# A first quarter in three pieces, and dummy products among the token transposes

## The chip, the core and the metric

The kernel runs on one core of a Trainium2 chip. The core has a matrix engine (PE, with its own loader of stationary operands, PEld), a vector engine (DVE), an activation engine (ACT), a general engine (POOL) and a queue engine (SP); SP, ACT and POOL can issue DMAs, which sixteen DMA engines carry out. The metric is the time of one execution in microseconds (us). Three executions of the kernel before took 2226.09, 2226.78 and 2231.04 us; the median is 2226.78 us.

## What is computed

One step of a two-layer trunk for 128 prompt tokens and 512 sample tokens with 2048 features. In each layer every token is normalised, scaled and shifted by a modulation that depends on its group's conditioning vector, sent through one wide input projection, a mixer, and an output projection:

```python
def modulation(cond, w, b):
    m = jax.nn.silu(cond) @ w + b
    ...
    return jnp.split(m, 3, axis=-1)
...
    for layer in range(DEPTH):
        sh_p, sc_p, gt_p = modulation(c_ctx, ada_w[layer], ada_b[layer])
        sh_s, sc_s, gt_s = modulation(c, ada_w[layer], ada_b[layer])
        hp = rms_norm(xp, norm_g[layer]) * (1.0 + sc_p) + sh_p
        hs = rms_norm(xs, norm_g[layer]) * (1.0 + sc_s) + sh_s
        ...
            out_p, (kc, vc) = even_mixer(hp, *w)
            out_s, _ = even_mixer(hs, *w, ctx=(cache_a_k[:, i], cache_a_v[:, i]), rope=rope)
```

`ada_w` has 2048 x 6144 numbers a layer: columns 0 to 2047 give the shift, the next 2048 the scale, the last 2048 the gate. So the first product of the input projection cannot start before the tokens are transposed, their norms are known, and at least some columns of `ada_w[0]` have been read and multiplied with the two conditioning vectors.

## The kernel before

**Layout.** Tokens stand along the free dimension (640 columns: 512 sample and 128 prompt tokens), features along the 128 partitions; the 2048 features are 16 feature tiles, four of which are a quarter (`qd`). A wide product of the projection takes three passes (weights high by tokens high, high by low, low by high; lines 364 to 366), each over 320 tokens, so a feature tile costs one output tile six matmuls.

**The start.** `x_load` fetches the tokens in five blocks of two halves (line 120), on ACT's queue and SP's. `x_block` (line 1072) sends each block through PE: four transposes fill one PSUM bank `T` (line 1078; two such banks in turn), DVE or, for the last of the four groups of every other block, ACT copies it to `xT` (line 1079), and ACT squares and sums the block's halves for the norms (line 1083). POOL raises the sums to the power -1/2, and `x_rows` spreads them (lines 1093 and 1094).

**Conditioning.** `ada_on_pe(l, cb, j0, n)` makes `n` feature tiles of column block `cb` of the modulation: 16 weight tiles with 32 x (n*128) products (line 195) into a bank `T`, a copy by ACT to `ada_sb` (line 198), `n` transposes (line 201), and a few small DVE instructions (lines 203, 179, 168). Its weights come through `ada_t`, two buffers of 4096 numbers a partition, or, given `spare`, through the places of token tiles that are no longer needed (`adah`). Block `4 + g` is the scale and block `g` the shift of quarter `g`.

**The leading tiles.** `run_tiles` (line 421) starts with six output tiles at once, the leads, in the order 0, 1, 3, 2, 4, 5. Leads 1 and 2 stay in PSUM; leads 0, 3, 4 and 5 (`trans`) share one pair of banks (`pa`, `pb`), and after each unit of features ACT (first unit, line 457) or DVE (later units, line 459) moves or adds the pair to a sum in SBUF. A unit is a run of features; before, `cut=((0, 2), (2, 4))` makes two units of 256 features of each quarter, eight in all. For every unit, `load_raw` (line 341) fetches each lead's weights into one of four buffers `raw`, the first unit's first four by SP, all others by POOL; `split_w` makes the high part on ACT (`wh`, line 328) and the low part on DVE (`wl`, line 329), four buffers each. `make_h` builds the unit's normalised and modulated tokens (`ht` by DVE, the high part by ACT, the low part by DVE; lines 1117 to 1122), and `proj_q` (line 356) does the products. After the second lead of a unit, `ahead` calls `ada_group` for the next unit, which queues its conditioning weights and products.

**What sets the order.** Each engine does its instructions in one fixed order. That order is made before the run by a scheduler that works from its own estimates; the code order is only a guide to it. At run time an instruction waits for the semaphores of what it reads and of the buffers it takes over, and everything behind it on its engine waits too. A DMA that SP issues also waits for the DMA eight before it among SP's and ACT's.

Of the kernel before, what the change touches and what calls it, by code (L numbers as in the profile page):

```python
# [20 lines left out]
P = 128  # L21
# [22 lines left out]
ORDER_X = (0, 2, 1, 3, 4)  # L44

SPARE = {4: (15, 14, 11, 10), 0: (13, 12, 9, 8), 5: (15, 14, 11, 10), 1: (13, 12, 9, 8), 6: (15, 14, 13, 12)}
# [8 lines left out]
def trunk_kernel(ctx: ExitStack, tc: tile.TileContext, I: dict, O: dict):  # L55
    nc = tc.nc
    V, A, PE, G = nc.vector, nc.scalar, nc.tensor, nc.gpsimd
# [22 lines left out]
    def bank(tag, name):  # L80
        return (pproj if tag[-1] == "0" else pools["more", "at"]).tile([P, 512], F32, tag=tag, name=name)
# [7 lines left out]
    def psT():  # L89
        return pT.tile([P, 512], F32, tag="T", name="T")  # L90

    def load_rows(dst, name):
        nc.sync.dma_start(dst, I[name][0].partition_broadcast(P))
# [14 lines left out]
    sT = const.tile([P, KT, 32], F32, name="sT")  # L108
# [27 lines left out]
    ada_t = [pre.tile([P, 4096], F32, name=f"ada{i}") for i in range(2)]  # L136
# [18 lines left out]
    ones = const.tile([P, 32], F32, name="ones")  # L155
# [7 lines left out]
    def ada_done(l, cb, j0=0, n=4):  # L163
        fs = slice(cb * 4 + j0, cb * 4 + j0 + n)
        which, k0 = cb // 4, (cb % 4) * 4 + j0
        ks = slice(k0, k0 + n)
        if which == 1:
            V.scalar_tensor_tensor(out=gsc[l][:, ks, :], in0=mod[l][:, fs, :], scalar=1.0,
                                   in1=norm_g[l][:, ks][:, :, None].to_broadcast([P, n, 2]),
                                   op0=ALU.add, op1=ALU.mult)  # L170
        elif which == 2:
            V.tensor_scalar(hgt[l][:, ks, :], mod[l][:, fs, :], 0.5, None, ALU.mult)
# [4 lines left out]
    def add_bias(l, cb, red, j0=0, n=4):  # L177
        fs = slice(cb * 4 + j0, cb * 4 + j0 + n)
        V.tensor_tensor(mod[l][:, fs, :], red, ada_b[l][:, fs][:, :, None].to_broadcast([P, n, 2]), op=ALU.add)

    def ada_on_pe(l, cb, j0=0, n=4, spare=()):


        acc, m, wd = psT(), 4 if spare else 32 // n, n * P
        for i, kt in enumerate(range(KT)):
            if kt % m == 0:
                if spare:
                    w = hpool.tile([P, m, wd], F32, tag=f"h{spare[kt // m]}", name="adah")
                else:
                    w = ada_t[0].rearrange("p (k n) -> p k n", k=m)  # L190
                    ada_t.reverse()
                nc.sync.dma_start(w, I["ada_w"][l, kt * P:(kt + m) * P, cb * 512 + j0 * P:cb * 512 + j0 * P + wd]
                                  .rearrange("(k p) n -> p k n", p=P))
            g = kt % 4
            PE.matmul(acc[32 * g:32 * g + 32, 0:wd], sT[:, kt, :], w[:, kt % m, :],  # L195
                      start=(i < 4), stop=(i >= KT - 4), tile_position=(0, 32 * g))
        sb = ada_sb
        A.copy(sb[:, 0:wd], acc[:, 0:wd])
        tr = psT()
        for j in range(n):  # L200
            PE.transpose(tr[:, j * P:(j + 1) * P], sb[:, j * P:(j + 1) * P], ident)
        red = small.tile([P, n, 2], F32, tag="red", name="red", bufs=2)
        V.tensor_reduce(red, tr[:, 0:wd].rearrange("p (b g c) -> p b c g", b=n, g=4)[:, :, 0:2, :], axis=AX.X,
                        op=ALU.add)
        add_bias(l, cb, red, j0, n)
        ada_done(l, cb, j0, n)
# [214 lines left out]
    def run_tiles(jobs, w_ap, make_h, fill=None, rate=0.0, ahead=None, order=(0, 1, 2, 3), before=None,  # L421
# [9 lines left out]
        else:  # L431
# [2 lines left out]
        pps = {n: (sums[n][:, 0:HALF], sums[n][:, HALF:NT]) if n in trans  # L434
               else new_pp(lead_pp[n] if lead_pp else 1 + held.index(n) if trans else n ^ flip if n < 2 else n)
               for n in leads}
        units = [(pos, qd, js) for pos, qd in enumerate(order) for js in (cut or [(0, 4)])]
        for ui, (pos, qd, js) in enumerate(units if leads else ()):
            queue = nc.gpsimd if trans and ui else None
            raws = {n: load_raw(w_ap, jobs[n][0], qd, js, queue) for n in leads[:W_BUFS] if ui or n not in early}  # L440
# [65 lines left out]
        t = 0  # L506
        if before:
            settle()
        elif pending:
            n = pending.pop(0)  # L510
            begin(jobs[n][1], pps[n])
        for i in range(lead, len(jobs)):
# [18 lines left out]
            for qd in range(4):  # L531
# [15 lines left out]
                if pending and not prep:  # L547
                    n = pending.pop(0)
# [523 lines left out]
    def x_block(b, ts):  # L1072
        s4 = small.tile([P, 2], F32, tag="s4", name="s4")
        for g in range(4):
            ta = psT()
            for j in range(4):
                o = g % 2 * 512 + j * P
                PE.transpose(ta[:, j * P:(j + 1) * P], ts[g // 2][:, o:o + P], ident)
            (A.copy if g == 3 and b % 2 == 0 else V.tensor_copy)(xT[g][:, :, b * P:(b + 1) * P],
                                                  ta.rearrange("p (j t) -> p j t", j=4))  # L1080
            if g % 2 == 0:
                junk = pS.tile([P, 1024], F32, tag="S", name="sqj")
                A.activation(junk, ts[g // 2], AF.Square, accum_out=s4[:, g // 2:g // 2 + 1])
        ss = small.tile([P, 1], F32, tag="nm", name="ssx")
        V.tensor_reduce(ss, s4, axis=AX.X, op=ALU.add)
        V.tensor_scalar(ss, ss, 1.0 / D, EPS, ALU.mult, ALU.add)
        G.tensor_tensor(rx[:, b:b + 1], ss, half[:, 0:1], op=ALU.pow)

    def x_rows(bs):

        t = psT()
        for i, b in enumerate(bs):
            PE.matmul(t[:, i * P:(i + 1) * P], rx[:, b:b + 1].to_broadcast([P, P]), ident, start=True, stop=True)
        A.copy(rows[:, bs[0] * P:(bs[-1] + 1) * P], t[:, 0:len(bs) * P])

    def ada_group(g, js):
        for cb in (4 + g, g):
            ada_on_pe(0, cb, js[0], js[1] - js[0], SPARE.get(cb, ()) if js[0] else ())
        if g == 3 and js[1] == 4:
            for i, n in enumerate(("a_k_norm", "c_k_norm", "d_k_norm")):  # L1100
                load_rows(gain_rows[:, i, :], n)
            nc.sync.dma_start(band, I["k_band"])
            load_rows(sink, "a_sink")

    for i, b in enumerate(ORDER_X):
        x_block(b, xs[b])
        if i == 3:
            cond_in()
    ada_on_pe(0, 4, 0, 2)
    x_rows((0, 1, 2, 3))  # L1110
    x_rows((4,))

# [14 lines left out]


    def keep(ui, n, pp):
        g = {(6, 0): 0, (6, 4): 1, (7, 0): 2, (7, 4): 3}.get((ui, n))  # L1130
        if g is not None:
            V.tensor_copy(xTm[g][:, 4 * NT:4 * NT + 1], pp[1][:, 0:1])
            nc.gpsimd.dma_start(x0dram[g][:, 0:4 * NT + 1], xTm[g][:, 0:4 * NT + 1])
# [346 lines left out]
    def twist():  # L1480
        drain(attn)
        for j in range(8):
            hi, lo = hs[j]
            split(hi[:, HALF:NT], lo[:, HALF:NT], t1[j])
        st.pop("adaw")

    used = run_tiles(jobs, I["ev_w_in"][0], h0_maker, fill0, FILL0, ada_group, trans=TRANS, grace=GRACE,
                     cut=((0, 2), (2, 4)), summed=keep, led=even_start, lead_in=lambda: ada_on_pe(0, 0, 0, 2),
                     steps=lambda i: 0.4 if i >= n_turn else 1.35 if i > last_q else 1.1,
                     turn=(n_turn, fill0b, 0.7, tail_turn), twist=twist, fill_from=FILL0_FROM)  # L1490

# [341 lines left out]
    busy = set()  # L1833
# [306 lines left out]
```

## Time and profile before

| | before |
|---|---|
| median of three executions | 2226.78 us |
| profiled execution | 2223.7 us |
| its span, first to last instruction | 2221.9 us |
| PE busy in the span | 2191.2 us (99%) |
| DVE, ACT, POOL busy | 78%, 51%, 12% |
| first transpose of tokens | 4.74 us |
| first product of the projection | 35.12 us |
| DMA in the first 40th of the span | 367 GB/s |
| DMA over the span | 166 GB/s |

All times of the profile count from the start of the span. A row of the timeline gives the start, the time from start to the end of the last of the merged instructions, engine, line, operation, output<-input, sizes, the count, and in brackets how long the engine had been idle and what ended that. A matmul in 32-bit floats is recorded as two instructions, so 16 products read x32. The ends of matmuls are modelled, and a matmul's row reaches past the start of the next one; the distance of two starts tells what it costs. In the table of windows each engine's busy time is followed by its number of instructions, then come the clock that PE was granted (1.00 is full), the share of the DMA engines, and GB/s.

### The profile page before, as it was taken

How to read it: one execution, taken by the hardware profiler on the slowest of the kernel's cores; microseconds unless marked ns; L12 is line 12 of the kernel's file. 1: busy time of each engine (PE TensorE's matmuls, PEld its weight loads, DVE VectorE, ACT ScalarE, POOL GpSimd, SP SyncE). 2: the span in 40 equal slices, each digit the busy share in tenths (PEclk: the TensorE clock that was granted, in tenths of full speed). 3: DMA queues.
4: the chain of work that ended last, by engine and by line, in shares of the span. 5: the costliest groups of instructions: out<-in, count | busy, mean ns of one | idle time of the engine just before them, and what ended most of it. 6: DMA issues, size and time to landing. Idle time of an engine off the chain costs nothing.

```text
span 2221.9 us, 40941 instructions
## 1 busy us (share of the span) xinstructions
PE 2191.2 (99%) x15456; PEld 2121.7 (95%) x15456; DVE 1738.2 (78%) x3031; ACT 1134.9 (51%) x2421; POOL 256.2 (12%) x409
## 2 busy tenths in 40 slices
PE   7999999999999999999999999999999999999999
PEld 5899999999999999999999999999999999999998
DVE  5659898989888977877787878978567567677875
ACT  4334453535334445444654466555578766663343
POOL 3221000000100100000111112211010011111110
PEclk9999999999999999999999999999999999999999
DMA  9985556565453435844674434544523233347641
GB/s 367 340 291 176 171 164 209 179 196 165 149 160 120 144 102 175 259 125 133 218 250 154 147 99 124 168 147 147 180 81 104 70 99 118 120 137 240 213 142 51
DMA packets 380373, 368.44 MB, mean 166 GB/s; under 512 B 18946, under 2 KB 326624, under 8 KB 379664
## 3 DMA queue, kind: packets, MB, share of 16 engines
q1 hardware_dynamic: 357248, 284.78, 41.5%
q0 software_dynamic: 22064, 78.83, 9.9%
q8 instruction: 121, 1.98, 0.3%
q10 hardware_dynamic: 864, 2.23, 0.3%
q14 instruction: 76, 0.62, 0.1%
HBM read 312.41 MB, written 48.11 MB: 162 GB/s over the span
## 4 chain that ended last, share of the span: by engine, by line
PE 90%; DVE 3%; DMA 3%; issue 2%; ACT 2%; POOL 1%; SPq 0%; ACTq 0%; DVEq 0%; POOLq 0%
PE pq L667 13%; PE pq L669 13%; PE pq L668 13%; PE pa L364 6%; PE pa L365 6%; PE pa L366 6%; PE pb L364 6%; PE pb L366 5%; PE pb L365 5%; PE T L915 2%; PE S L927 1%; PE T L195 1%; PE S L928 1%; PE S L929 1%; PE T L697 1%
## 5 line engine op out<-in xcount | busy, mean ns | idle before, releaser
L328 ACT ACTIVATE wh<-raw 128x512 fp32r<-128x512 f32 (+1 forms) x352 | 210.5, 600 | 322.7 <-PE pb L365 202.6
L667 PE MATMUL pq<-h,wh 128*128 128x320 f32 x1152 | 358.6, 311 | 0.0
L669 PE MATMUL pq<-h,wl 128*128 128x320 f32 x1152 | 356.3, 309 | 0.1
L668 PE MATMUL pq<-h,wh 128*128 128x320 f32 x1152 | 356.1, 309 | 0.0
L364 PE MATMUL pa<-h,wh 128*128 128x320 f32 x944 | 299.5, 318 | 0.3 <-ACT h L1121 0.2
L365 PE MATMUL pa<-h,wh 128*128 128x320 f32 x944 | 295.4, 313 | 3.3 <-DVE h L329 3.2
L364 PE MATMUL pb<-h,wh 128*128 128x320 f32 x944 | 294.6, 313 | 0.0
L366 PE MATMUL pb<-h,wl 128*128 128x320 f32 x944 | 293.2, 311 | 0.2 <-DVE wl L329 0.2
L366 PE MATMUL pa<-h,wl 128*128 128x320 f32 x944 | 293.4, 311 | 0.0
L365 PE MATMUL pb<-h,wh 128*128 128x320 f32 x944 | 292.6, 310 | 0.0
L329 DVE TENSOR_TENSOR wl<-raw,wh 128x512 fp32r<-128x512 f32 (+1 forms) x352 | 228.2, 649 | 75.4 <-ACT wh L328 71.2
L667 PE MATMUL pq<-T,wh 128*128 128x320 f32 x864 | 268.8, 311 | 0.0
L669 PE MATMUL pq<-T,wl 128*128 128x320 f32 x864 | 267.1, 309 | 0.4 <-DVE wl L329 0.4
L668 PE MATMUL pq<-T,wh 128*128 128x320 f32 x864 | 267.0, 309 | 0.0
L328 ACT ACTIVATE wh<-sx 128x512 fp32r<-128x512 f32 x216 | 135.7, 632 | 182.1 <-PE pq L668 114.5
L667 PEld LDWEIGHTS pq<-h,wh 128*128 128x128 f32 x1152 | 216.4, 188 | 2.1 <-issue 2.1
L669 PEld LDWEIGHTS pq<-h,wl 128*128 128x128 f32 x1152 | 216.2, 188 | 0.3 <-DVE wl L329 0.3
L668 PEld LDWEIGHTS pq<-h,wh 128*128 128x128 f32 x1152 | 216.4, 188 | 0.0
L282 DVE SCALAR_TENSOR_TENSOR acc<-adaw,sT,acc 128x1024 f32<-128x1024 f32 x150 | 188.9, 1275 | 0.0
L364 PEld LDWEIGHTS pa<-h,wh 128*128 128x128 f32 x944 | 177.7, 188 | 10.2 <-issue 8.7
L365 PEld LDWEIGHTS pa<-h,wh 128*128 128x128 f32 x944 | 178.2, 189 | 8.9 <-issue 4.7
L329 DVE TENSOR_TENSOR wl<-sx,wh 128x512 fp32r<-128x512 f32 x216 | 147.6, 688 | 43.1 <-ACT wh L328 39.5
(426 smaller groups left out, 4953.0 us busy)
## 6 DMA issues: line engine op xcount, KB each, us to landing
adaw<-in_ada_w SPq DMA_DIRECT2D x80, 512.0 KB, 4.1
raw<-in_ev_w_in SPq DMA_DIRECT2D x130, 256.0 KB, 3.4
raw<-in_od_w_in SPq DMA_DIRECT2D x112, 256.0 KB, 3.2
w<-in_od_w_in SPq DMA_DIRECT2D x48, 512.0 KB, 4.1
ada<-in_ada_w SPq DMA_DIRECT2D x11, 2048.0 KB, 12.5
adaw<-in_ada_w POOLq DMA_DIRECT2D x69, 256.0 KB, 3.4
w<-in_ev_w_in SPq DMA_DIRECT2D x27, 512.0 KB, 3.7
adah<-in_ada_w SPq DMA_DIRECT2D x20, 512.0 KB, 9.3
```

The lines of the kernel that those rows point to most:

```text
L195: PE.matmul(acc[32 * g:32 * g + 32, 0:wd], sT[:, kt, :], w[:, kt % m, :], start=(i < 4), stop=(i >= KT - 4), tile_position=(0, 32 * g))
L282: V.scalar_tensor_tensor(out=acc[c], in0=w, scalar=sT[:, kt, c:c + 1], in1=acc[c], op0=ALU.mult, op1=ALU.add)
L328: A.activation(hi, x, AF.Copy)
L329: V.tensor_sub(lo, x, hi)
L364: PE.matmul(ps, wh[:, i, :], hi[:, sl], start=(j == js[0] if alone else (pos == 0 and j == 0)), stop=False)
L365: PE.matmul(ps, wh[:, i, :], lo[:, sl], start=False, stop=False)
L366: PE.matmul(ps, wl[:, i, :], hi[:, sl], start=False, stop=(j == js[1] - 1 if alone else (pos == 3 and j == 3)))
L667: PE.matmul(ps, wh[:, j, :], hi, start=(first and h == 0 and j == 0), stop=False, skip_group_check=True)
L668: PE.matmul(ps, wh[:, j, :], lo, start=False, stop=False, skip_group_check=True)
L669: PE.matmul(ps, wl[:, j, :], hi, start=False, stop=(final and h == 1 and j == 3), skip_group_check=True)
L697: PE.transpose(t[:, i * P:(i + 1) * P], src(b), ident)
L915: PE.transpose(t[:, i * P:(i + 1) * P], p, ident)
```

## The change

Three things change. The first quarter is taken in three units of 128, 128 and 256 features instead of two of 256, and the conditioning weights for the first two are fetched and multiplied 128 columns at a time: one DMA of 1 MB with runs of 512 bytes where there was one of 2 MB with runs of 1024 bytes, into one half of a buffer `ada_t`. The other quarters keep two units. Three dummy products of `ones` with `sT` (512 columns, 32-bit) go to a PSUM bank that is otherwise unused then: two ahead of the first transposes, one after the second group of the first block. The keys in `keep`, which write `xT` out, move by one because there is one unit more.

```diff
-        acc, m, wd = psT(), 4 if spare else 32 // n, n * P
+        acc, m, wd = psT(), 4 if spare else 16 if n == 1 else 32 // n, n * P
...
-                    w = ada_t[0].rearrange("p (k n) -> p k n", k=m)
+                    w = ada_t[0][:, j0 % 2 * m * wd:(j0 % 2 + 1) * m * wd].rearrange("p (k n) -> p k n", k=m)
...
-        units = [(pos, qd, js) for pos, qd in enumerate(order) for js in (cut or [(0, 4)])]
+        units = [(pos, qd, js) for pos, qd in enumerate(order) for js in (cut[qd] if cut else [(0, 4)])]
...
+            if b == ORDER_X[0] and g == 1:
+                keep_busy(1)
...
-            ada_on_pe(0, cb, js[0], js[1] - js[0], SPARE.get(cb, ()) if js[0] else ())
+            ada_on_pe(0, cb, js[0], js[1] - js[0], SPARE.get(cb, ()) if js[0] == 2 else ())
...
+    def keep_busy(n):
+        t = bank("pb1", "busy")
+        for _ in range(n):
+            PE.matmul(t[0:32, :], ones, sT.rearrange("p k c -> p (k c)"), start=True, stop=True)
+
+    keep_busy(2)
...
-    ada_on_pe(0, 4, 0, 2)
+    ada_on_pe(0, 4, 0, 1)
...
-        g = {(6, 0): 0, (6, 4): 1, (7, 0): 2, (7, 4): 3}.get((ui, n))
+        g = {(7, 0): 0, (7, 4): 1, (8, 0): 2, (8, 4): 3}.get((ui, n))
...
-                     cut=((0, 2), (2, 4)), summed=keep, led=even_start, lead_in=lambda: ada_on_pe(0, 0, 0, 2),
+                     cut=[((0, 1), (1, 2), (2, 4))] + [((0, 2), (2, 4))] * 3, summed=keep, led=even_start,
+                     lead_in=lambda: ada_on_pe(0, 0, 0, 1),
```

The order of the instructions changes in the first 307 of PE's products before, which are the first 342 after (three dummy products and 32 narrow conditioning products more); behind them every engine's order is word for word that of before, apart from line numbers. Three places show what moved.

The first place is ACT's order while the last token blocks come in (`sqj` are the squares of a half block, `xT` the copy of a transposed group, `wh` the high part of a lead's weights, `ada_sb` the copied conditioning products). Before:

```order
L1083 ACTIVATE sqj,s_312<-xb 128x1024 x2
L1083 ACTIVATE sqj,s_345<-xb 128x1024 x2
L1083 ACTIVATE sqj,s_386<-xb 128x1024
L328 ACTIVATE wh<-raw 128x256
L1083 ACTIVATE sqj,s_386<-xb 128x1024
L1079 COPY xT_244<-T 128x4x128
L328 ACTIVATE wh<-raw 128x256 x3
L198 COPY ada_sb<-T 128x256
```

And now, from the third block's squares on:

```order
L1083 ACTIVATE sqj,s_317<-xb 128x1024 x2
L328 ACTIVATE wh<-raw 128x128
L1083 ACTIVATE sqj,s_350<-xb 128x1024
L328 ACTIVATE wh<-raw 128x128
L1083 ACTIVATE sqj,s_350<-xb 128x1024
L328 ACTIVATE wh<-raw 128x128
L1083 ACTIVATE sqj,s_391<-xb 128x1024
L328 ACTIVATE wh<-raw 128x128
L1083 ACTIVATE sqj,s_391<-xb 128x1024
L1079 COPY xT_244<-T 128x4x128
L198 COPY ada_sb<-T 128x128
```

The first split of weights stood behind nine of the ten squares and now stands behind six.

The second place is PE's order around the first product of the projection (`ada` and `adah` are conditioning weights, `rx` the norms). Before:

```order
L195 MATMUL T<-ada_125,sT 32x256 x16
L201 MATMUL T<-ident,ada_sb 128x128 x2
L1093 MATMUL T<-ident,rx 128x128 x5
L195 MATMUL T<-ada_126,sT 32x256 x16
L201 MATMUL T<-ident,ada_sb 128x128 x2
L195 MATMUL T<-adah,sT 32x256 x8
L364 MATMUL pa<-h_515,wh 128x320 x2
```

And now:

```order
L195 MATMUL T<-ada_125,sT 32x128 x16
L201 MATMUL T<-ident,ada_sb 128x128
L1095 MATMUL T<-ident,rx 128x128 x5
L195 MATMUL T<-ada_126,sT 32x128 x16
L201 MATMUL T<-ident,ada_sb 128x128
L195 MATMUL T<-ada_125,sT 32x128 x16
L364 MATMUL pa<-h_518,wh 128x320 x2
```

Each of the two conditioning steps ahead of the first product is half as wide, and a third narrow one has taken the place of the first eight products of the next unit.

The third place is ACT's order where the first unit ends and the second begins (`sum` is an SBUF sum of a lead, copied from `pa` and `pb`; `h` the high part of a feature tile). Before, from the copies of the second lead in `pa`/`pb`:

```order
L457 COPY sum_458<-pa 128x320
L328 ACTIVATE wh<-raw 128x256
L457 COPY sum_458<-pb 128x320
L198 COPY ada_sb<-T 128x256
L328 ACTIVATE wh<-raw 128x256
L1121 ACTIVATE h_718<-ht_128,mod_132 128x512
L1121 ACTIVATE h_718<-ht_128,mod_132 128x128
L457 COPY sum_459<-pa 128x320
```

And now, from the same copies:

```order
L457 COPY sum_462<-pa 128x320
L457 COPY sum_462<-pb 128x320
L328 ACTIVATE wh<-raw 128x128 x2
L1129 ACTIVATE h_662<-ht_129,mod_132 128x128
L457 COPY sum_463<-pa 128x320
L328 ACTIVATE wh<-raw 128x128
L457 COPY sum_463<-pb 128x320
L457 COPY sum_464<-pa 128x320
L328 ACTIVATE wh<-raw 128x128
L457 COPY sum_464<-pb 128x320
```

The splits that stand between the copies of the last two leads are now those of the second unit's third and fourth lead.

## The prediction

> **What bounds the kernel now.** I read the page first, then the windows of the start, the chain of waits, and the timeline of each engine up to the first product of the projection.
>
> ```profile
> PE 2191.2 (99%) x15456; PEld 2121.7 (95%) x15456; DVE 1738.2 (78%) x3031; ACT 1134.9 (51%) x2421; POOL 256.2 (12%) x409
> ```
>
> PE is busy for 2191.2 of 2221.9 us, so a microsecond is won or lost only where PE waits, or where it is given more to do. The windows show where it waits:
>
> ```profile
> 10.00:20.00 10.00, 8.26 (x36) 6.07 (x34) 5.05 (x11) 5.16 (x10) 2.06 (x4) 1.00 1.05 399
> 40.00:50.00 10.00, 10.00 (x82) 7.49 (x81) 4.98 (x14) 4.17 (x11) 2.84 (x4) 1.00 1.08 385
> 169.50:172.90 3.40, 0.80 (x6) 0.61 (x6) 3.09 (x7) 1.90 (x6) 0.63 (x1) 1.00 0.55 183
> 172.90:176.30 3.40, 3.40 (x15) 3.40 (x14) 3.40 (x7) 2.76 (x8) 0.00 (x0) 0.50 0.53 153
> ```
>
> From 40 us on PE is full but for a gap near 170. The change lies in the first 60 us, where the DMA engines run at their limit (shares of 1.05 to 1.08). Behind that the order of every engine is unchanged, so whatever PE has gained or lost by then it carries to the end. The chain of waits names PE in the start as well:
>
> ```profile
> 12.54 1.13 PE T L1078 x4
> ...
> 23.69 0.66 PE T L1078 x4
> ...
> 53.41 1.86 PE T L195 x32
> ```
>
> Four transposes take 1.13 us early and 0.66 us later: PE runs at half speed until about 19 us, although the profile's column of the clock shows 1.00. The third row gives the price of 16 conditioning products of 256 columns in a full stream, 1.86 us.
>
> **The head, up to the first product.** PE's own chain:
>
> ```profile
> 4.74 1.97 PE L1078 MATMUL T<-ident,xb 128*128 128x128 f32 x8 [4.74 <-DMA xb<-in_x_sample]
> 8.77 2.98 PE L1078 MATMUL T<-ident,xb 128*128 128x128 f32 x12 [2.06 <-DMA xb<-in_x_sample]
> ...
> 26.55 1.93 PE L195 MATMUL T<-ada,sT 128*32 128x256 f32 x32
> 28.98 0.44 PE L201 MATMUL T<-ident,ada_sb 128*128 128x128 f32 x2 [0.49 <-ACT ada_sb L198]
> 29.25 1.28 PE L1093 MATMUL T<-ident,rx 128*128 128x128 f32 x10
> 30.98 1.93 PE L195 MATMUL T<-ada,sT 128*32 128x256 f32 x32 [0.45 <-ACT tables L1094]
> 33.84 1.07 PE L195 MATMUL T<-adah,sT 128*32 128x256 f32 x16
> 35.12 0.56 PE L364 MATMUL pa<-h,wh 128*128 128x320 f32 x2 [0.22 <-ACT h L1121]
> ```
>
> It looks as if warm transposes would pull all of this forward by 4 us. They don't, because of ACT, whose order now puts the first split of weights behind six squares, and so makes it wait for those weights:
>
> ```profile
> 25.12 0.40 ACT L328 ACTIVATE wh<-raw 128x256 fp32r<-128x256 f32 x1
> 25.43 1.01 ACT L1083 ACTIVATE sqj<-xb 128x1024 f32<-128x1024 f32 x1
> 26.38 0.19 ACT L1083 ACTIVATION_READ_ACCUMULATOR sqj<-xb 128x1 f32 x1
> 26.47 0.59 ACT L1079 COPY xT<-T 128x512 f32<-128x512 f32 x1
> ```
>
> ```profile
> 8.16 0.33 SPq L120 DMA_DIRECT2D xb<-in_x_prompt  x1
> 8.65 0.39 SPq L192 DMA_DIRECT2D ada<-in_ada_w  x1
> 11.14 8.61 SPq L341 DMA_DIRECT2D raw<-in_ev_w_in  x4
> ```
>
> ```profile
> xb<-in_x_prompt SPq DMA_DIRECT2D x1, 512.0 KB, 9.2
> ada<-in_ada_w SPq DMA_DIRECT2D x1, 2048.0 KB, 14.2
> raw<-in_ev_w_in SPq DMA_DIRECT2D x1, 128.0 KB, 12.1
> ```
>
> The first rows are ACT's, the next SP's issues, the last the sizes and times to landing of those three issues, for the raw loads of the first of four. SP's transfers land one after the other: the last token block at 8.16 + 9.2 = 17.4, the 2 MB of conditioning weights at 8.65 + 14.2 = 22.85, the first raw load at 11.14 + 12.1 = 23.24. So 2 MB in runs of 1024 bytes take 5.5 us, and 128 KB in runs of 512 bytes 0.39 us, 3.1 us a MB. After the change the conditioning weights are 1 MB in runs of 512 bytes and land at 17.4 + 3.1 = 20.5, the first raw load of 64 KB at 20.7. From 8.8 us, when the first block's second half is there, ACT has five squares, two copies of 0.59 and a small instruction ahead of that split and waits a little for the transposes, so it gets there at about 17.5 and stands for 3 us. Then come four splits and four squares. A square is 1.14 to 1.18 us (25.43 to 26.57 with its sum read out); a split of 128x128 is about 0.3, taken from the 0.40 of 128x256. That is 5.9 us: the last square ends at 26.6, the copy at 27.2. Before, they ended at 26.57 and 27.06. What the dummies and the earlier weights win is lost in this wait.
>
> The dummies cost nothing: PE idles before the first transposes (4.74 us) and before the third group (2.06), and if two cold products of 512 columns (the 1.28 us of five 128-column ones at full clock make it 1 to 2 us each) hold up the first block by a microsecond, ACT's wait covers it. Without that cover it would be 1 us.
>
> From the first conditioning product on, which again starts at about 26.6, the chain is shorter: each of two products is 16 x 128 columns for 16 x 256, half of 1.93, so 1.9 us less for both; two copies of 0.37 become about 0.27; two transposes of 0.1 fall out. Together 2.2 us, so the first product stands at 32.9. If narrow products were paced by instruction and not by columns, they would save nothing, the head would win 0.3 us and the work below grow by 0.9; I take the halving, since transposes of 128 columns, four in 0.66 us with their tail, show no floor above it.
>
> **Work that moves behind the first product.** Before, 24 of the 64 conditioning products of the first quarter were still to do after it (1.5 x 1.86 = 2.8 us); now 16 narrow and 32 wide ones are (0.93 + 3.72 = 4.65 us), and two more transposes. PE has 2.1 us more to do in a stretch where it was full. Head and work nearly cancel: -0.1 us.
>
> **Waits for weights.** What remains is new. A unit of 128 features gives each lead six matmuls, but still needs six raw loads through four buffers:
>
> ```profile
> 36.60 0.31 PE L366 MATMUL pb<-h,wl 128*128 128x320 f32 x1
> 36.75 0.31 PE L364 MATMUL pb<-h,wh 128*128 128x320 f32 x1
> ```
>
> ```profile
> raw<-in_ev_w_in POOLq DMA_DIRECT2D x12, 128.0 KB, 5.6
> ...
> raw<-in_ev_w_in POOLq DMA_DIRECT2D x3, 128.0 KB, 2.5
> ```
>
> ```profile
> L329 DVE TENSOR_TENSOR wl<-raw,wh 128x256 fp32r<-128x256 f32 x48 | 20.0, 420 | 9.5 <-ACT wh L328 9.5
> L459 DVE TENSOR_TENSOR sum<-sum,pb 128x320 f32<-128x320 f32 x26 | 12.6, 485 | 6.2 <-PE pb L366 6.1
> L457 ACT COPY sum<-pa 128x320 f32<-128x320 f32 x4 | 1.7, 421 | 3.2 <-PE pa L366 3.2
> ```
>
> A raw load issued by POOL in the first 60 us lands after 5.6 us; where the DMA engines are half idle (139 to 143 us) it takes 2.5. With a split by ACT and one by DVE of about 0.3 each a buffer comes round in 6.3 us, four in 1.6 us apiece. Six matmuls at 0.147 us (320 columns; 12 matmuls made a lead before, 1.76 us) are 0.88 us. So the two narrow units outrun their loads.
>
> First place: the second unit's third load takes the buffer of the first unit's fifth. Lead 0's products end at about 34.5 (eight matmuls and two small pieces behind 32.9), ACT's two copies of 0.42 at 35.3, the fifth split at 35.9 with DVE's part; the load issued then lands at 41 to 41.5, and ACT splits it, by its order, ahead of copying lead 4's second bank. The bank is free at 41.7. PE wants it, after some 33 matmuls, a half-size and a small piece of conditioning, at about 39.7. Wait: 2.0 us.
>
> Second place: the second unit's sixth load is split when PE has let go of a `wh` buffer, at about 48, behind the 32 conditioning products of the third unit; the third unit's fourth load follows in its buffer at 48.9 and lands at 54.5. PE arrives at 53.3: 1.6 us, then 0.9 for the tokens' low parts that DVE does behind that split, and 0.5 for banks, since eight more additions of 0.485 us come in. Wait: 3.0 us.
>
> Together 5.0 us. The lower end is nothing, if 64 KB land after 2.5 us; the upper 7, if each load is 1 us later. I take 5.6 us a load, because the DMA engines are as full then as in the stretch it is from.
>
> The DMAs: the four narrow conditioning loads make 4 MB at 3.1 instead of 2.75 us a MB, 1.4 us more. The next ones are used about 4 us after they land, and PE itself is late by then, so this is hidden; were that slack gone, it would cost its 1.4.
>
> **Sum.** -2.2 (head) + 2.1 (work) + 5.0 (waits) = +4.9 us. The profiled execution took 2223.7 us, 1.8 outside the span, and would take 2228.6; the median of the three is 3.1 us above it, which I keep: 2226.8 + 4.9 = 2231.7. Within 0.2%, 4.5 us, a measurement of this kernel can hardly tell a difference from none.
>
> **The rivals.** (1) The loads keep up. If 64 KB from POOL land in 2.5 us, each place loses its 2 to 3 us: -0.1 us, 2226.7. Against it speak the full DMA engines. The Trainium skill (DMA: Bandwidth & Descriptors, Anatomy of one DMA) gives such a load 2.0 us plus its bytes at 436 GB/s, an estimate of 2.2 us here, so by its rule this rival holds; the trace's 5.6 us in this stretch disagrees.
>
> (2) Faster. If the first raw load landed by 17.5, ACT would not stand, the head would win another 3.1 us, and with no waits behind it the sum is -3.2: 2223.6. It decides at a landing 3 us earlier than the queue allows, since the last token block itself lands at 17.4. To be faster by over 0.2%, the half clock after the idle window at 169.5 would have to fall away as well; its 15 instructions would take 2.2 us at 0.147, so it costs 1.2.
>
> (3) Waits that cost clock. The window from 169.50, with PE busy for 0.80 of 3.40 us, is followed by 3.4 us at a granted clock of 0.50. If the two waits of 2 to 3 us do the same, each costs 1.2 to 1.7 us more (half of 3.4 at most): 2233 to 2235. The Trainium skill (TensorE: Matmul & The Clock Gate, The HAM clock gate) lets the clock fall only after an idle window of about 3.4 us; by that rule these waits cost no clock and the sum stays. The trace already shows a fall after a window that was a quarter busy.
>
> (4) The dummies do not warm PE. Then transposes run at 1.13 a group up to 19 us as before, mostly under ACT's wait: some 0.4 us more, 2232.1, inside the forecast's own range.
>
> **Chances.** The forecast 0.60 (its own range 2229 to 2234, (4) in it), rival 1 0.20, rival 2 0.05, rival 3 0.15. Over 2231.2 lie three fifths of the forecast and rival 3: slower 0.52. Faster by over 0.2% needs rival 2 and more: 0.05. Within: 0.43. The range from 2226 to 2235 leaves out rival 2 and the ends, 2 in 10.
>
> **What would show it.** The first product at about 33; ACT idle for 3 us ahead of its first split, ended by a raw load; the last square at 26.6; PE idle near 40 to 42 and 53 to 56 behind splits that wait for raw loads; transposes at 0.66 from about 9 us. If ACT doesn't stand, or raw loads land within 4 us, I am too slow; if the clock falls between 40 and 60, too fast.

## The result and the profile after

The changed kernel takes 2236.67 us (median of seven executions, 2232.78 to 2239.65) against 2226.78 us before (seven, 2221.29 to 2231.04): a ratio of 1.0043, with a 95% interval of 1.0032 to 1.0055, so 9.6 us slower (7.1 to 12.2). The profiled execution took 2236.67 us with a span of 2234.8. That is 13.0 more than the profiled execution before, which happened to lie 3.1 under its median; so the stages are compared by a mark in the trace and not by the two spans. The mark is the start of one group of sixteen conditioning products, behind the last difference in PE's order. Its rows in PE's timeline, of before and of after:

```profile
99.60 1.93 PE L195 MATMUL T<-adah,sT 128*32 128x256 f32 x32
```

```profile
108.18 1.93 PE L195 MATMUL T<-adah,sT 128*32 128x256 f32 x32
```

PE is 8.6 us late there: most of the loss is made in the first 100 us. The other 4.3 of the 13.0 us come later in this execution, where the order is that of before: the clock falls once more at 1121 us, where it is full before, and what decides this stays open. The first part of the page, and the windows of the stage:

```profile
PE 2198.7 (98%) x15526; PEld 2123.6 (95%) x15526; DVE 1743.8 (78%) x3050; ACT 1136.0 (51%) x2429; POOL 258.8 (12%) x415
```

```profile
20.00:30.00 10.00, 5.92 (x59) 4.58 (x59) 3.98 (x18) 5.92 (x14) 3.50 (x6) 0.83 1.11 331
...
40.00:50.00 10.00, 8.24 (x81) 4.90 (x79) 3.95 (x13) 2.75 (x10) 3.21 (x5) 1.00 1.08 388
50.00:60.00 10.00, 7.66 (x48) 5.51 (x46) 7.09 (x19) 3.96 (x10) 3.55 (x5) 0.98 1.08 389
60.00:70.00 10.00, 10.00 (x93) 6.71 (x92) 4.49 (x12) 1.67 (x5) 1.43 (x2) 0.85 1.08 387
```

Where PE was full from 40 us on, it now lacks 1.8 and 2.3 us in two windows, and the clock is not full in three. The head first, in the timelines of ACT, DVE and PE:

```profile
21.13 0.31 ACT L328 ACTIVATE wh<-raw 128x128 fp32r<-128x128 f32 x1 [3.47 <-DMA raw<-in_ev_w_in]
...
26.57 0.59 ACT L1079 COPY xT<-T 128x512 f32<-128x512 f32 x1 [0.38 <-PE T L1078]
```

```profile
23.75 0.15 DVE L1087 TENSOR_REDUCE ssx<-s 128x1 f32<-128x2 f32 x1 [3.33 <-ACT sqj L1083]
...
24.08 1.28 DVE L1079 COPY xT<-T 128x512 f32<-128x512 f32 x2
```

```profile
24.82 1.71 PE L1078 MATMUL T<-ident,xb 128*128 128x128 f32 x8 [3.62 <-DVE xT L1079]
26.46 1.94 PE L195 MATMUL T<-ada,sT 128*32 128x128 f32 x32
...
30.69 1.08 PE L195 MATMUL T<-ada,sT 128*32 128x128 f32 x32 [0.45 <-ACT tables L1096]
...
33.74 0.56 PE L364 MATMUL pa<-h,wh 128*128 128x320 f32 x2 [0.20 <-ACT h L1129]
```

ACT stands 3.47 us ahead of its first split, for a raw load. DVE's sum of the fourth block's squares stands ahead of its copies of the last block, so those wait for ACT as well, and PE, with both banks `T` in use, waits 3.62 us for the copies. Behind that PE runs at half speed: the same narrow group takes 1.94 us at 26.46 and 1.08 at 30.69. The first product comes at 33.74, only 1.4 us earlier than before. Then the two waits, in ACT's and PE's timelines:

```profile
42.63 0.31 ACT L328 ACTIVATE wh<-raw 128x128 fp32r<-128x128 f32 x1 [2.23 <-DMA raw<-in_ev_w_in]
...
56.89 0.42 ACT L328 ACTIVATE wh<-raw 128x256 fp32r<-128x256 f32 x1 [1.70 <-DMA raw<-in_ev_w_in]
```

```profile
41.24 0.31 PE L366 MATMUL pa<-h,wl 128*128 128x320 f32 x1
43.31 0.41 PE L364 MATMUL pb<-h,wh 128*128 128x320 f32 x1 [1.75 <-ACT sum L457]
...
55.27 0.41 PE L364 MATMUL pa<-h,wh 128*128 128x320 f32 x1
57.35 0.41 PE L364 MATMUL Sp<-h,wh 128*128 128x320 f32 x1 [1.67 <-ACT wh L328]
57.60 0.31 PE L364 MATMUL pb<-h,wh 128*128 128x320 f32 x1
58.48 0.41 PE L365 MATMUL pa<-h,wh 128*128 128x320 f32 x1 [0.57 <-DVE h L1130]
```

Since the ends of matmuls are modelled, a wait is counted from start to start, less the 0.15 us that such a product takes in a full stream. The first product behind a gap takes 0.25 us (57.35 to 57.60), and the 0.1 more is counted with the gap. That is 2.0 us at the first place; at the second 2.04, 0.84 and 0.62 in small gaps from 53.3 on, 3.5 in all. Last the clock, in windows that follow its own steps of 3.41 us:

```profile
21.96:25.37 3.41, 0.55 (x4) 0.42 (x4) 1.62 (x6) 3.41 (x10) 0.68 (x2) 1.00 1.07 323
25.37:28.79 3.42, 3.03 (x38) 2.12 (x37) 1.45 (x6) 1.68 (x4) 2.77 (x5) 0.50 1.14 349
...
56.10:59.51 3.41, 1.59 (x8) 1.18 (x8) 2.18 (x5) 0.42 (x1) 0.72 (x1) 1.00 1.08 395
59.51:62.92 3.41, 3.41 (x19) 1.77 (x22) 1.42 (x4) 0.42 (x1) 0.00 (x0) 0.50 1.08 386
62.92:66.34 3.42, 3.42 (x41) 2.62 (x34) 0.88 (x4) 0.62 (x2) 0.71 (x1) 1.00 1.09 385
```

After these windows, in which PE was busy for 0.55 and 1.59 of 3.41 us, it gets half the clock for a window. From 59.51 it does 19 instructions where the next window holds 41: about 1.8 us lost.

### The profile page after: what moved, and what is told of

Read it like the earlier page. It is cut to its first block, busy times and chain, and to the rows that moved or that the text cites. A ratio compares the mean times of both kernels' runs of the same rounds, so it can differ in the third digit from the quotient of the medians.

```text
span 2234.8 us, 41139 instructions
## 1 busy us (share of the span) xinstructions
PE 2198.7 (98%) x15526; PEld 2123.6 (95%) x15526; DVE 1743.8 (78%) x3050; ACT 1136.0 (51%) x2429; POOL 258.8 (12%) x415
## 5 line engine op out<-in xcount | busy, mean ns | idle before, releaser
L328 ACT ACTIVATE wh<-raw 128x512 fp32r<-128x512 f32 (+2 forms) x358 | 211.9, 593 | 330.8 <-PE pb L365 209.7
L329 DVE TENSOR_TENSOR wl<-raw,wh 128x512 fp32r<-128x512 f32 (+2 forms) x358 | 229.7, 642 | 74.2 <-ACT wh L328 69.9
L329 DVE TENSOR_TENSOR wl<-sx,wh 128x512 fp32r<-128x512 f32 x216 | 147.9, 689 | 43.3 <-ACT wh L328 39.7
```

The costliest lines, as they stand in the source:

```text
L328: A.activation(hi, x, AF.Copy)
L329: V.tensor_sub(lo, x, hi)
```

## The experiments

Theory A: the raw loads come late, in the head and behind the first product, and the idle time they make takes the clock as well. Theory B: the stage is bound by the full DMA engines and the pieces of conditioning, so PE would wait for something else in any case. Theory C: the dummy products, which give PE its full clock early, do the harm (in the later runs: win nothing). Every edit also lets the scheduler make the order anew, so a run can differ from the changed kernel in more than its edit; where that matters it is said. The table has for every run the start of the first product, PE's waits over 0.5 us between it and 70 us (idle time), the times at which the clock fell between 20 and 70 us, how late the mark stands against 99.60, and the ratio to before with its interval.

| run | first product | waits behind it | clock falls | mark | ratio |
|---|---|---|---|---|---|
| before | 35.12 | none | none | 0 | 1 |
| changed | 33.74 | 1.75, 1.67, 0.57 | 25.4, 59.5 | +8.6 | 1.0043 (1.0032 to 1.0055) |
| e1 dummies alone | 35.67 | none | none | +0.5 | 0.9995 (0.9986 to 1.0003) |
| e2 cut alone | 31.74 | 1.66, 0.86, 0.56 | 42.4 | +5.6 | 1.0039 (1.0025 to 1.0052) |
| e3 raw in pairs | 34.92 | none | 22.5 | +4.0 | 1.0032 (1.0019 to 1.0045) |
| e4 first raw by POOL | 29.75 | 1.00, 1.94, 0.79 | 42.0 | +3.7 | 1.0011 (1.0003 to 1.0020) |
| e5 pairs, by POOL | 32.04 | none | 29.7 | +0.6 | 1.0011 (1.0001 to 1.0020) |
| e6 dummies, raw by POOL | 36.35 | none | 24.7 | +0.7 | 1.0006 (0.9997 to 1.0014) |
| e7 as e5, no dummies | 32.97 | none | none | +0.5 | 1.0008 (0.9999 to 1.0016) |
| e8 changed again | 33.79 | 1.85, 1.54, 0.56 | 25.3, 59.4 | +8.5 | 1.0043 (1.0030 to 1.0056) |
| e9 hold the head | 34.32 | 1.85 | none | +5.0 | 1.0031 (1.0020 to 1.0042) |
| e10 hold the waits | 33.38 | 0.60 | 24.8 | +5.0 | 1.0021 (1.0012 to 1.0031) |
| e11 raw ahead | 29.62 | 2.44 | none | +0.3 | 1.0013 (1.0004 to 1.0022) |
| e12 raw ahead, no dummies | 33.47 | none | none | +1.4 | 1.0002 (0.9993 to 1.0011) |

**e1 and e2: each half of the change alone.** e1 adds the dummies to the kernel before, e2 takes them out of the changed one:

```diff
+            if b == ORDER_X[0] and g == 1:
+                keep_busy(1)
...
+    keep_busy(2)
```

> The three dummy products on the kernel before, nothing cut. Theory A (the cut costs the time: waits for raw loads, 5.0 us counted from start to start, a half clock from 59.5 to 62.9 that follows them, about 1.9, and about 2.9 of conditioning work moved behind the first product, less 1.4 in the head): full clock from about 5 us, first product 0.5 to 1.5 us earlier than at 35.12, no wait behind it, 0.5 to 1.5 us faster than before. Theory C (the early clock is the harm: PE, full early, loses it in the head and later): a half clock window between 20 and 30 us and a time 1 to 3 us slower than before.

> The three pieces without the dummy products. Theory A: the waits of about 2 us near 43 and near 57 are there as with the dummies, and it is 8 to 11 us slower than before. Theory C: without the dummies no half clock in the first 65 us, and 4 to 6 us slower than before.

The dummies alone change the time by nothing that can be told. The clock is full early (eight transposes take 1.07 us at 8.73), but the first product comes 0.5 us later and not earlier: the head then waits for its second 2 MB of conditioning weights, as PE's timeline shows:

```profile
31.50 1.93 PE L195 MATMUL T<-ada,sT 128*32 128x256 f32 x32 [2.26 <-DMA ada<-in_ada_w]
```

The cut alone is slower by 8.7 us (5.6 to 11.6), so theory C falls for the whole. But in the trace it is 3.0 us better than with the dummies at the mark, and 2.0 of that at the first product. Its ACT and PE rows:

```profile
21.03 0.31 ACT L328 ACTIVATE wh<-raw 128x128 fp32r<-128x128 f32 x1 [0.79 <-DMA raw<-in_ev_w_in]
```

```profile
24.62 1.08 PE L195 MATMUL T<-ada,sT 128*32 128x128 f32 x32 [0.19 <-DVE ssx L1086]
...
31.74 0.56 PE L364 MATMUL pa<-h,wh 128*128 128x320 f32 x2 [0.20 <-ACT h L1126]
...
40.94 0.41 PE L364 MATMUL pb<-h,wh 128*128 128x320 f32 x1 [1.66 <-ACT sum L457]
```

The raw load lands at the same time, 21.0; the slower transposes only bring ACT there later, so it stands 0.79 us. Two of DVE's copies of the last block stand ahead of the fourth block's sums here, PE has no gap over 1.1 us, keeps its clock and takes 1.08 us for the group that took 1.94. Whether the medians differ by as much is not settled: the two intervals overlap.

**e3: one raw load for both narrow units.**

```diff
-            raws = {n: load_raw(w_ap, jobs[n][0], qd, js, queue) for n in leads[:W_BUFS] if ui or n not in early}
+            two = bool(trans) and ui < 2
+            if not two or ui == 0:
+                raws = {n: load_raw(w_ap, jobs[n][0], qd, (0, 2) if two else js, queue) for n in leads[:W_BUFS] if ui or n not in early}
...
-                        proj_q(pp, parts[n], qd, pos, alone=True, js=js)
+                        proj_q(pp, parts[n], qd, pos, alone=True, js=js, base=0 if two else None)
```

> The changed kernel, but the first two units share one raw load, one split and one set of buffers of 256 features for each lead (six buffers, the last two apart). Theory A: no PE wait over 0.5 us between the first product and 70 us, no half clock there, and 5 to 8 us faster than the changed kernel, so 2 to 5 slower than before. Theory B (the pieces of conditioning and the full DMA engines cost the time, the buffers only decide where PE stands): waits as long elsewhere before 100 us, and within 2 us of the changed kernel.

Both waits and the clock's fall behind them are gone, as A said and B did not, and the mark moves from 8.6 to 4.0 although the head lost 1.2 us (PE idles 4.64 us there, the first loads being twice as large). The time gained only 2.5 us, of 5 to 8 expected. The difference is made later, in ACT's timeline of this run:

```profile
159.16 1.17 ACT L328 ACTIVATE wh<-raw 128x512 fp32r<-128x512 f32 x2 [5.92 <-DMA raw<-in_ev_w_in]
```

There the first ordinary tiles' raw loads travel beside the writes of `x0d` (1280.5 KB each), and PE idles 4.82 us for them at 161.05. Waits of 0.5 to 2 us stand between 139 and 167 us in the changed kernel and in most other runs with the cut, and none over 0.2 before. What decides them stays open: the order there is that of before.

**e4: the first raw loads by POOL.**

```diff
-            queue = nc.gpsimd if trans and ui else None
+            queue = nc.gpsimd if trans else None
```

> The changed kernel, with the first unit's first four raw loads issued by POOL at about 5 us in place of SP behind the conditioning weights. Theory A: ACT does not stand ahead of its first split, PE keeps its clock between 20 and 30 us, the first product comes at 30 to 31.5 us and not at 33.74, the waits near 43 and 57 stay in sum: 1.5 to 4 us faster than the changed kernel. Theory B: the first product stays within 1 us of 33.7, since the token blocks or the conditioning weights come no earlier.

POOL issues the loads from 9.05 us on. ACT no longer stands ahead of its first split, no clock is lost in the head, and the first product comes at 29.75, 4.0 us earlier; the waits stay (1.94 and 0.79) and a new one of 1.00 for conditioning weights comes at 31.71. It is 7 us faster than the changed kernel (1.0011 for 1.0043), more than the 1.5 to 4 expected; the mark explains 4.9 of it, the rest is within the intervals.

**e5, e6 and e7: both cures, with and without the dummies; POOL loads without the cut.** e5 joins the edits of e3 and e4, e7 takes the dummies out of e5, e6 has e4's line on e1.

> The changed kernel with both cures: raw loads of 256 features shared by the first two units, and the first unit's raw loads issued by POOL. Theory A (raw loads are late in the head and behind the first product, and the idle time takes the clock): first product at 29.5 to 31 us, no PE wait over 1 us up to 70 us, no half clock there; the products at 62 us of the kernel before come 0.5 to 3 us earlier than there, and the time is 1 to 4 us under before. Theory B (the stage is bound by the DMA engines, and PE waits for conditioning weights in place of raw loads): 2 us or more of waits for conditioning weights between 29 and 60 us, and no faster than with the POOL loads alone, 2 us over before.

> The kernel before with the dummy products and the first unit's first raw loads by POOL, uncut. Theory A: ACT does not stand, but the second 2 MB of conditioning weights now end the head: they come some 1.5 us earlier than at 31.5 (the 0.5 MB of raw loads no longer ahead of them), the first product at about 34.2, 0.5 to 2 us faster than before. Rival (ACT's wait alone held the head with the dummies): first product at 32 to 33 us, 2 to 4 us faster than before.

> As the run with both cures, without the dummy products. Theory A: the transposes stay at half speed to about 19 us, and the first product comes 1 to 2 us later than with the dummies, 0.5 to 2 us slower than with them. Theory C (the dummies win nothing): first product within 0.5 us of the run with them, same time.

With no raw load late, the loss of 8.6 at the mark is down to 0.6 and 0.5: the raw loads account for nearly all of it. But no gain is left. e7 is the cleanest: its first product comes 2.15 us earlier than before, there is no wait and no fall of the clock, and the mark is 0.5 us late. So the work moved behind the first product is 2.15 + 0.48 = 2.6 us. With the dummies (e5) the first product comes 0.9 us earlier still, but the mark and the time are the same. e5 misses A's expectation (32.04 for 29.5 to 31; no gain): it fetches 0.75 MB of raw weights early, and its head waits for conditioning weights, as B expected (though 1.5 us and not 2 or more), and runs at half speed behind 29.66:

```profile
30.18 1.94 PE L195 MATMUL T<-ada,sT 128*32 128x128 f32 x32 [1.47 <-DMA ada<-in_ada_w]
```

In e6 the same stands ahead of both wide groups (1.53 and 1.50 us); its first product is later than either expectation. The first 2 MB of conditioning weights, issued at 8.7 us, take 15.8 us to land there and 14.7 in e1, without the early raw loads.

**e8: the changed kernel again.** No edit.

> The changed kernel once more, for another phase of the clock's windows of 3.41 us. If the clock falls when more than about half of one window is idle, it falls behind the wait near 43 or the one near 57 only where that wait lies mostly in one window: the waits are the same to 0.3 us, and at 62 us of the kernel before the products are 8.7 us late with one fall, 6.8 with none, 10.5 with two. If a wait as such takes the clock, the half clock stands at 59.5 again and 8.7 us again.

The waits and the mark come again to 0.3 us (row in the table). The clock's windows happened to lie as in the first profile, so this run does not tell the two readings apart.

**e9 and e10: PE kept busy in its idle time.** e9 in the head, e10 ahead of the two waits:

```diff
+            if b == ORDER_X[-1] and g == 1:
+                keep_busy(4)
```

```diff
+                    if trans and (ui, n) in ((0, leads[5]), (1, leads[5])):
+                        for _ in range(3):
+                            PE.matmul(pps[1][0][0:30, 0:HALF], sT[:, 0, 2:32], xT[3][:, 0, 0:HALF], start=False, stop=False)
```

> The changed kernel with four more dummy products where PE idles for 3.62 us ahead of the last transposes. If the idle time takes the clock there (theory A): no half clock between 20 and 32 us, the last eight transposes in 1.25 us and not 1.71, the first narrow conditioning group in 1.08 and not 1.94, the first product at 32.2 to 32.9 and not 33.74, though PE has more to do; about 1 us faster than the changed kernel. If something else lowers it (the clock falls at a set time after the start, or with the load of the chip), the half clock stays at 25 us and the first product at 33.7 or later.

> The changed kernel with three products of zero weights (0.5 us each, added into a lead's bank that is open then) ahead of each of the two waits, 3.2 us of work more. Theory A (the wait ends when the weights are there, whatever PE does until then, and an idle PE loses its clock): the two waits shrink by 1 to 1.6 us each, no half clock between 40 and 63, and the products at 62 us of the kernel before are 6.5 to 7.5 us late and not 8.7, the time 1 to 2 us under the changed kernel. If the waits are bound to PE's own pace, they stay near 2 us, and it is 3 us slower than the changed kernel.

The clock follows PE's idle time in both: in the head it does not fall in e9, where PE was kept busy, and in e10, where it was not, it still falls at 24.8. PE's rows of e9 and of e10:

```profile
21.99 2.76 PE L1112 MATMUL busy<-sT,ones 128*32 128x512 f32 x6
25.42 0.65 PE L1078 MATMUL T<-ident,xb 128*128 128x128 f32 x4 [0.67 <-DVE xT L1079]
...
27.89 1.08 PE L195 MATMUL T<-ada,sT 128*32 128x128 f32 x32 [0.50 <-DVE xT L1079]
```

```profile
39.95 1.80 PE L454 MATMUL pa<-xT,sT 128*30 128x320 f32 x6
...
42.98 0.41 PE L364 MATMUL pb<-h,wh 128*128 128x320 f32 x1 [0.60 <-ACT sum L460]
```

In e9 the group takes 1.08 us, but it starts 1.4 us later (the raw load lands 0.6 later, and the copies come behind it), so the first product is 34.32 and not the 32.2 to 32.9 expected: the head was bound by ACT and its load, and a full clock alone doesn't buy it back. Still e9 is 2.7 us faster than the changed kernel (the intervals overlap), and 3.6 us better at the mark, since the second wait is gone and with it the half clock behind it. e10 does 3.5 us more of useless work (two rows of 1.80 us, some 1.7 each in the stream) and is 5 us faster than the changed kernel, more than expected: the first wait shrank as its work grew, the clock stayed full behind both places, and the second wait vanished.

That the second wait is gone in e9 and e10 is the scheduler's doing. The raw load is late as in the changed kernel; this is ACT's row of e9:

```profile
57.54 0.42 ACT L328 ACTIVATE wh<-raw 128x256 fp32r<-128x256 f32 x1 [2.52 <-DMA raw<-in_ev_w_in]
```

But the new order puts more products that don't need this split ahead of those that do, among them nine conditioning products of the next unit in e9, and PE works through them meanwhile (in e10 the three dummies too). So what the late load costs PE depends on what the order puts ahead of its split.

**e11 and e12: raw loads ahead, in a place of their own.** e4's line, and the second unit's raw loads go where the last token block's half was, on POOL's queue from about 24 us; e12 leaves out the dummies.

```diff
+        if own:
+            if ownr[0] is None:
+                ownr[0] = hpool.tile([P, 6, P], F32, tag="h6", name="late")
+            raw = ownr[0][:, ownr[1]:ownr[1] + 1, :]
+            ownr[1] += 1
...
+            own = own_pool if trans and ui == 1 else None
```

> The changed kernel with the first unit's first four raw loads by POOL at about 5 us, and the second unit's six raw loads in a place of their own (that of the last token block's half) from about 22 us, so that they do not wait for the first unit's buffers; the splits keep their four buffers and their order. Theory A (the three pieces lose by late raw loads alone; without them the earlier first product less 2.8 us of work moved behind it is what is left): first product at 29.7 to 30.5 us, waits near 40 and 57 under 0.7 us each, up to 1.2 us of waits for conditioning weights near 31, the landmark group 0 to 2 us earlier than in the kernel before, and 0 to 3 us faster than it. Theory B (whatever is loaded earlier delays something else by as much, since the DMA engines are full until 80 us): waits for conditioning weights of 2 us or more between 30 and 60 us, the landmark 1 to 4 us later than before.

> The same without the dummy products. Theory A: first product 0.5 to 1.5 us later than with them (cold transposes), the landmark within 1 us of the kernel before, and the same time as before within 0.1%. Theory C (the dummies win nothing): first product within 0.3 us of the run with them.

e11 has the earliest head of all and no wait near 40 or 57, and gains nothing (0 to 3 us were expected):

```profile
29.62 0.56 PE L372 MATMUL pa<-h,wh 128*128 128x320 f32 x2 [0.20 <-ACT h L1140]
...
33.04 0.38 PE L195 MATMUL T<-ada,sT 128*32 128x128 f32 x2 [2.44 <-DMA ada<-in_ada_w]
```

The first product is 5.5 us earlier than before; 2.6 of that goes to the work behind it, 2.6 (2.72 from start to start) to the wait for the next conditioning weights, and the rest, with the 0.3 by which the mark is late, to gaps too small to be listed. So A holds for the raw loads, and B for what is left. e4 is the run to compare with: up to the mark PE, ACT and DVE do the same instructions in the same order there, and only the second unit's raw loads are issued at other times and to another place. In e4 PE waits 1.94 and 0.79 us near 40 and 57 and the clock falls at 42.0; in e11 there is neither. But PE got these conditioning weights at 31.71 in e4:

```profile
31.71 0.38 PE L195 MATMUL T<-ada,sT 128*32 128x128 f32 x2 [1.00 <-DMA ada<-in_ada_w]
```

So while the DMA engines are full, the raw loads that come earlier made these weights 1.3 us later. The mark is 3.4 us better than in e4, but the times do not show it (1.0013 for 1.0011). e12's expectation on the head held less well (33.47, 3.9 us later than e11 instead of 0.5 to 1.5), and its mark, 1.4 late, lies outside the 1 us expected. So here the dummies do bring the head forward; by the mark it is 1.1 us, and in the times nothing of it is seen (1.0002 in e12, 1.0013 in e11, with intervals that overlap). No kernel tried is faster than the one before.

## Why the prediction was right and wrong

It had the direction, slower, and the places; the size was half: 4.9 us forecast, 9.6 measured (7.1 to 12.2), and 2236.67 lies outside the range of 2226 to 2235. The step that failed is the sum itself: it added the waits and left out the clock that their idle time takes.

| step | forecast | shown |
|---|---|---|
| head | -2.2 | -1.4 |
| work moved behind the first product | +2.1 | +2.6 |
| first wait | +2.0 | +2.0 |
| second wait | +3.0 | +3.5 |
| clock lost behind the second wait | not in the sum | +1.8 |
| sum, against the mark | +4.9 | +8.5 of 8.6 |

**The waits for weights** were right in place and cause, and near in size (the second is 0.5 us longer): ACT by its order splits a late load ahead of the copy that frees a bank, and buffers come round too slowly for units of 128 features. e3 and e11 take the late loads away and the waits go, in e11 against e4 with nothing else in the order changed. That the first wait has just the forecast size is partly luck: PE was ready at 41.4 us for 39.7 forecast, and the load was split at 42.6 for 41 to 41.5, both later. At the second place the order has its part as well, as e9 shows, where the same late load costs PE nothing. Rival 1, that the loads keep up, is refuted: a 64 KB raw load by POOL took 5.1 us between 30 and 62 us, in the profile's list of DMA issues:

```profile
raw<-in_ev_w_in POOLq DMA_DIRECT2D x4, 64.0 KB, 5.1
```

So the 5.6 us taken from larger loads in the same stage was near. The estimate of 2.2 us that the prediction gave from the Trainium skill (DMA: Bandwidth & Descriptors, Anatomy of one DMA) does not hold while the engines are full; the trace decides.

**ACT's stand in the head** came as told: it reached its split at 17.7 and got it at 21.13 (17.5 and 20.7 forecast), and the last copy stood at 26.57 to 27.16 (27.2). The step that failed in the head is the next one, "each of two products is 16 x 128 columns for 16 x 256, half of 1.93": the first group took 1.94, since PE had idled through the stand and ran at half speed. The second took 1.08. The halving by columns was right; the clock was missing, 0.9 us, which accounts for the error of this term (0.8).

**The failing step of the sum** is that the clock stood outside it. Rival 3 had the mechanism (a mostly idle window costs the next one half its speed) and priced it at 1.2 to 1.7 us for each wait, but at a chance of 0.15. It took place in the head, which the rival didn't name, and behind the second wait: 0.9 + 1.8 = 2.7 of the 3.7 us between forecast and mark. e9 shows for the head that idle time is its cause, and e4 and e11 show it for a wait near 40 us: in the same order the clock falls with the wait and not without it. Behind the second wait of the changed kernel it is read from the windows. Rival 3 with the forecast gave 2233 to 2235; the right sum would have been its upper end and a little more.

**The work moved** was taken as columns alone. e7 has it by itself at 2.6 us, 0.5 more than forecast. With that and the second wait's 0.5 the account closes to 0.1 us at the mark. The prediction's "whatever PE has gained or lost by then it carries to the end" holds for the medians within their interval (9.6, from 7.1 to 12.2, for 8.6), but not for single executions, whose later stretches differ by several microseconds in the same order (e3 by 6.0 between the mark and 194 us).

**The dummies cost nothing** holds for the kernel before (e1) and not for the changed one, where by the traces they cost 3.0 us at the mark (e2). Their cover was said to be ACT's wait; but PE, made early by them, idles 3.62 us in that wait, where without them it has no gap over 1.1 us, and so loses the clock. That they give the full clock early held: eight transposes take 1.09 us at 5.20, for 1.97 at 4.74 before. And the conditioning loads' 1.4 us were hidden, as told: PE waits for none of them in the changed kernel, and of the kernels with the cut only in e4, e5 and e11, whose heads are earlier.

## What to carry to other kernels

When a change makes units smaller, count the loads and their time round the buffers, not the bytes: six loads of half the size, at the same 5 us each, starved two units. Put the clock into the sum and not among the rivals as soon as a wait of two microseconds is forecast, and ask of every wait taken away what will be late next: here the conditioning weights, so that even a first product 5.5 us earlier brought nothing.

## What was not expected of the hardware

The clock fell after far less idle time than one whole window. Here are two windows each of e2 and of e4, the first with the wait near 40 us, the second with the half clock behind it:

```profile
39.00:42.41 3.41, 1.75 (x15) 0.88 (x15) 0.94 (x3) 1.86 (x6) 0.84 (x2) 1.00 1.08 383
42.41:45.82 3.41, 3.41 (x25) 2.07 (x27) 1.18 (x3) 0.31 (x1) 1.42 (x2) 0.50 1.07 390
```

```profile
38.61:42.02 3.41, 1.48 (x14) 0.87 (x14) 0.58 (x2) 1.57 (x5) 0.72 (x1) 1.00 1.09 391
42.02:45.43 3.41, 3.41 (x25) 2.06 (x27) 1.18 (x3) 0.31 (x1) 1.42 (x2) 0.50 1.07 386
```

And the same wait in the changed kernel, where a border of the windows cuts it in two, and a window of e1:

```profile
39.03:42.45 3.42, 2.52 (x15) 1.66 (x13) 1.33 (x4) 1.37 (x6) 1.53 (x3) 1.00 1.08 380
42.45:45.86 3.41, 2.55 (x25) 1.68 (x29) 1.18 (x4) 1.89 (x6) 1.45 (x2) 1.00 1.08 387
```

```profile
27.06:30.47 3.41, 1.69 (x16) 1.37 (x12) 1.30 (x6) 1.13 (x3) 1.93 (x3) 1.00 1.09 387
```

PE busy for 1.48 or 1.75 us of 3.41 cost the clock, 1.69 (in e1) and 2.5 did not. With windows laid out in steps of 3.41 us from each trace's own falls, and once PE has first had its full clock, it fell after every window with PE busy for 1.59 us or less and after none with 2.0 or more. So the border is near half a window, but not sharp by this count: between 1.6 and 2.0 us the clock was mostly kept, but it fell in e2 above and here, in e3 and in e5:

```profile
19.06:22.47 3.41, 1.95 (x13) 1.14 (x11) 1.36 (x6) 0.25 (x1) 0.55 (x1) 1.00 1.05 309
```

```profile
26.25:29.66 3.41, 1.86 (x35) 1.25 (x35) 1.34 (x4) 1.60 (x4) 0.10 (x1) 1.00 1.13 356
```

What else counts stays open. It is the busy time of one window that counts, and so one and the same wait of two microseconds costs 1.8 us more or nothing, by where the windows lie in that execution. The Trainium skill (TensorE: Matmul & The Clock Gate, What's actually happening) has the windows run freely at 3413 ns, and the steps of 3.41 us here agree. Its section HAM oscillation — how this bites in real kernels gives as the rule that PE must not idle for more than about 3.4 us; these windows disagree, since idle times of 1.66 and 1.94 us were enough, and the measurement decides.
